# An SSD mixer's elementwise work is moved from GpSimd to VectorE and ScalarE, and its norm's sums to other banks

## The chip, the cores and the metric

The program runs on one core of a Trainium2 chip. The metric is device time in microseconds (us). In the profile PE is the matrix engine, PEld its weight load, DVE the vector engine, ACT the scalar engine, POOL is GpSimd, and SP issues most of the DMAs. Each engine takes its instructions in order; they wait for each other through semaphores.

## The reference

A two-layer decoder on 1040 tokens of 1024 channels (16 learned tokens and 1024 inputs). Layer 0 is a state-space mixer (SSD) with a gated norm, layer 1 an attention; a convolutional feed-forward stands behind each. All is float32. The mixer, cut:

```python
z, xbc, dt_raw = jnp.split(u @ w_in, [...], axis=-1)
xbc = jax.nn.silu(_causal_dwconv(xbc, conv_w, conv_b))          # width 4
xs, b_in, c_in = jnp.split(xbc, [...], axis=-1)                 # 4 groups, 8 heads each
dt = jax.nn.softplus(dt_raw + dt_bias)
xdt = x_c * dt_c[..., None]
a_cs = jnp.cumsum(dt * a, axis=-1)                              # per chunk and head
decay_in = jnp.exp(jnp.where(causal, a_cs[..., :, None] - a_cs[..., None, :], -jnp.inf))
y_diag = einsum('bclgn,bcsgn->...', c_c, b_c) * decay_in @ xdt
chunk_states = einsum(b_c, jnp.exp(a_cs[..., -1:] - a_cs), xdt)
state = state * chunk_decay + chunk_states                      # from chunk to chunk
y = y_diag + einsum(c_c, prev_state, jnp.exp(a_cs)) + xs * d_skip
hg = y * jax.nn.silu(z)                                         # per group of 512 channels
hg = hg * lax.rsqrt(jnp.mean(hg * hg, -1) + eps) * gate_g
h = h + hg @ w_out
```

## The kernel before

Every matmul in float32 is done as three products of rounded halves (`mm3`: hi by hi, hi by lo, lo by hi); the high half `wh` of a weight block comes from ACT, the low half `wl = w - wh` from another engine (`load_w`). Channels lie on the 128 partitions, tokens along the free axis in three tiles of 348, 348 and 344 (`TT`).

The mixer (0 to about 660 us of the span) first normalizes the input, makes `dt` and its running sums (`dt_path`, a generator whose steps are called between projection tiles) and projects group 0. Then four groups with nine chunks of 116 tokens each follow. For each chunk `ssd_decays` loads the running sums `D` (116 x 8 heads x 116) and `E`, takes differences and the exponential, and multiplies E by C; `ssd_front` makes C·B (`cb`), transposes x (`px`) and B (`pb`, copied by ACT to `bk`), and multiplies `xdt`, `D`, `xde`; `ssd_back` makes the chunk's state `S`, updates `state`, and makes `y`, which is added to x. Between a chunk's front and back stand tiles of projection work for the next groups, 24 products of 3 x 8 each (`stream`): the six conv blocks of the next group (`in_group`; a tile ends with ACT's L273 and three DVE L277, all reading the PSUM bank), and the four gate blocks of the present one (`gate_group`; ACT's silu reads the bank, then DVE multiplies). A block's weights are loaded when the block before it begins. When a group's gate blocks are through, its gated norm (`gate_norm`) is called once ahead of each of three tiles that follow: a matmul with ones sums the squares over channels into a bank `ms`, then come Ln, Exp, one Newton step on DVE, and four scalings.

PSUM has eight banks: `mm` has two and `ex` one, between which projection tiles rotate (the third tile of a block takes `ex`), `sm` has three (cb, pb, y, ms), `lg` two (px, S). A bank comes free when its last reader is done.

In this section the order of PE, DVE, ACT and POOL is the order in which the code is written (`manual_schedule`); SP's DMAs, and the rest of the kernel except the attention, are ordered by the framework's scheduler. Behind the section the output projection (`out_proj`, accumulators `acc`, result added to `h` on DVE) begins, and the last group's norm sums stand among its first products.

The norm's sums and steps, which several places share:

```python
def rstd(self, accs, n, width, y=None, table=True):            # L178
    if table:
        self.ln_exp()                                          # ACT table load
    ps = self.sm("ms")
    ... matmul(ps, ones, acc)                                  # L187
    nc.scalar.activation(y, ps, AF.Ln, scale=1.0 / width)      # L190
    nc.scalar.activation(y, y, AF.Exp, scale=-0.5)             # L191
    b = y * y; b = b * ps; b = -0.5 / width * b + 1.5; y = y * b   # DVE, L192 to L195
```

Of the kernel before, what the change touches and what calls it, by code (L numbers as in the profile page):

```python
# [8 lines left out]
F32 = mybir.dt.float32  # L9
F32R = mybir.dt.float32r  # L10
AF = mybir.ActivationFunctionType
ALU = mybir.AluOpType
# [30 lines left out]
SMB, LGB = 3, 2  # L43
DT0 = 0
LAG = 2

NW = 8
SUMS = ((6, 1), (3, 6), (7, 6), (3, 5), (5, 7)), ((4, 7), (2, 1))
# [19 lines left out]
class Trunk:  # L68
# [64 lines left out]
                                pattern=[[1, CB]], channel_multiplier=-1)  # L133


    def load_w(self, src, n, gain=None, pool=None, tags=("wh", "wl"), eng=None):
        nc = self.nc
        pool = pool or self.wp
        w32 = self.wp.tile([P, 1024], F32, tag="w32", name=self.nm("w32"))
        nc.sync.dma_start(w32[:, :n], src)  # L140
        if gain is not None:
            v = w32[:, :n].rearrange("p (k c) -> p k c", k=KD)
            g = gain.unsqueeze(2).to_broadcast([P, KD, n // KD])
            nc.gpsimd.tensor_tensor(v, v, g, op=ALU.mult)
        wh = pool.tile([P, 1024], F32R, tag=tags[0], name=self.nm("wh"))
        wl = pool.tile([P, 1024], F32R, tag=tags[1], name=self.nm("wl"))
        nc.scalar.activation(wh[:, :n], w32[:, :n], AF.Copy)
        (eng or nc.gpsimd).tensor_tensor(wl[:, :n], w32[:, :n], wh[:, :n].bitcast(F32), op=ALU.subtract)
        return wh, wl

    def mm3(self, out, wh, wl, uh, ul, first, last, joins=False):
# [363 lines left out]

    def gate_norm(self, g, x, acc, j):
        s0, n = TT[j]
        r = self.rstd([acc.pop(j)], n, DI // GROUPS)
        for q in range(4):
            xq = x[q][:, s0 : s0 + n]  # L520
            self.nc.vector.scalar_tensor_tensor(xq, xq, self.par("gate_norm", 4 * g + q), r, op0=ALU.mult, op1=ALU.mult)

    def settle(self):

# [30 lines left out]
    def ssd_decays(self, g, ct, c, pool):  # L555

        nc = self.nc
        h0 = GH * g
        t0, n = CH[c]
        cc = 3 * (c % 3) + c // 3  # L560
        dk = pool.tile([P, 1024], F32, tag="D", name=self.nm("D"))
        dk = dk[:n, : GH * CB].rearrange("p (h l) -> p h l", h=GH)
        nc.sync.dma_start(dk, self.acs_d[c, h0 : h0 + GH].unsqueeze(0).to_broadcast([n, GH, CB]))
        dk = dk[:, :, :n]
        ce = None
        if c:
            ce = pool.tile([P, GH * CB], F32, tag="E", name=self.nm("E"), bufs=2)
            ce = ce.rearrange("p (h l) -> p h l", h=GH)
            nc.sync.dma_start(ce, self.ea_d[c, h0 : h0 + GH].unsqueeze(0).to_broadcast([P, GH, CB]))
            ce = ce[:, :, :n]  # L570
        yield dk, ce

        for i in range(GH):
            nc.vector.tensor_scalar(dk[:, i], dk[:, i], self.cols[:n, 1, cc, h0 + i : h0 + i + 1], 0.0, op0=ALU.subtract, op1=ALU.min)
        nc.scalar.activation(dk, dk, AF.Exp)
        yield
        if c:
            nc.gpsimd.tensor_tensor(ce, ce, ct[:, t0 : t0 + n].unsqueeze(1).to_broadcast([P, GH, n]), op=ALU.mult)
        yield

    def ssd_front(self, g, x, bt, ct, c, dk, pool):

        nc = self.nc
        h0 = GH * g
        tt = nc.vector.tensor_tensor
        t0, n = CH[c]
        cc = 3 * (c % 3) + c // 3
        e = t0 + n
        pcb = self.sm("cb")
        nc.tensor.matmul(pcb[:n, :n], bt[:, t0:e], ct[:, t0:e], start=True, stop=True)  # L590
        px = self.lg("px")
        for q in range(4):
            nc.tensor.transpose(px[:n, q * P : q * P + P], x[q][:, t0:e], self.ident)
        px = px[:n].rearrange("p (h d) -> p h d", h=GH)
        cbm = pool.tile([P, CB], F32, tag="cbm", name=self.nm("cbm"), bufs=2)
        tt(cbm[:n, :n], pcb[:n, :n], self.past[:n, :n], op=ALU.mult)
        xdt = pool.tile([P, GH, 64], F32, tag="xdt", name=self.nm("xdt"), bufs=2)
        tt(xdt[:n], px, self.cols[:n, 0, cc, h0 : h0 + GH].unsqueeze(2).to_broadcast([n, GH, 64]), op=ALU.mult)
        tt(dk, dk, cbm[:n, :n].unsqueeze(1).to_broadcast([n, GH, n]), op=ALU.mult)
        bk = xde = None  # L600
        if c < 8:
            pb = self.sm("pb")
            nc.tensor.transpose(pb[:n, :P], bt[:, t0:e], self.ident)
            bk = pool.tile([P, P], F32, tag="bk", name=self.nm("bk"), bufs=2)
            nc.scalar.activation(bk[:n], pb[:n, :P], AF.Copy)
            xde = pool.tile([P, GH, 64], F32, tag="xde", name=self.nm("xde"), bufs=2)
            nc.gpsimd.tensor_tensor(xde[:n], xdt[:n], self.cols[:n, 2, cc, h0 : h0 + GH].unsqueeze(2).to_broadcast([n, GH, 64]), op=ALU.mult)
        return xdt, xde, bk

    def ssd_back(self, g, x, c, dk, ce, xdt, xde, bk, state, pool):  # L610

        nc = self.nc
        h0 = GH * g
        t0, n = CH[c]
        cc = 3 * (c % 3) + c // 3
        e = t0 + n
        new = None
        if c < 8:
            ps = self.lg("S")
            nc.tensor.matmul(ps, bk[:n], xde[:n].rearrange("p h d -> p (h d)"), start=True, stop=True)  # L620
            new = pool.tile([P, GH, 64], F32, tag="state", name=self.nm("state"), bufs=2)
            psv = ps.rearrange("p (h d) -> p h d", h=GH)
            if c == 0:
                nc.scalar.activation(new, psv, AF.Copy)
            else:
                nc.gpsimd.tensor_tensor(new, state, self.cd[:, cc, h0 : h0 + GH].unsqueeze(2).to_broadcast([P, GH, 64]), op=ALU.mult)
                nc.vector.tensor_tensor(new, new, psv, op=ALU.add)
        py = self.sm("y")
        for i in range(GH):
            q, r = i // 2, 64 * (i % 2)  # L630
            y = py[r : r + 64, q * CB : q * CB + n]
            nc.tensor.matmul(y, xdt[:n, i, :], dk[:, i, :], start=True, stop=c == 0)
            if c:
                nc.tensor.matmul(y, state[:, i, :], ce[:, i, :], start=False, stop=True)
        for q in range(4):
            nc.vector.scalar_tensor_tensor(x[q][:, t0:e], x[q][:, t0:e], self.par("d_skip", 4 * g + q),
                                           py[:, q * CB : q * CB + n], op0=ALU.mult, op1=ALU.add)
        return new

    def mixer(self, mx):  # L640
# [5 lines left out]
        with self.tc.tile_pool(name="ssd", bufs=3) as pool:  # L646
# [17 lines left out]
            into = lambda g: self.in_group(u, g, rows[g])  # L664
            blocks = into(1) + gate(0) + into(2) + gate(1) + into(3) + gate(2) + gate(3)
            for n, _ in enumerate(self.stream(into(0))):
                if n % 3 == 2:
                    next(dt, None)
                if n == 14:
                    w0 = self.load_w(blocks[0][0], D)  # L670
            work = self.stream(blocks, w0)
            E = mybir.EngineType
            with self.tc.manual_schedule(engines={E.PE, E.DVE, E.Activation, E.Pool}):
                ahead = self.ssd_decays(0, rows[0][5], 0, pool)
                dk, ce = next(ahead)
                for g in range(GROUPS):
                    *x, bt, ct = rows[g]
                    tiles, given = (18, 30, 30, 18)[g], 0
                    state = None
                    for c in range(9):  # L680
                        for _ in ahead:
                            pass
                        ops = self.ssd_front(g, x, bt, ct, c, dk, pool)
                        now = dk, ce
                        for _ in range((tiles * (c + 1) + 8) // 9 - given):
                            next(work)
                            if given == (tiles * c + 8) // 9:
                                nxt = (g, ct, c + 1) if c < 8 else (g + 1, rows[g + 1][5], 0) if g < 3 else None
                                ahead = self.ssd_decays(*nxt, pool) if nxt else iter([(None, None)])
                                dk, ce = next(ahead)  # L690
                            else:
                                next(ahead, None)
                            given += 1
                        state = self.ssd_back(g, x, c, *now, *ops, state, pool)
                        if g == 3:
                            done.append(c)
                            todo, waiting[:] = waiting[:], []
                            for w in todo:
                                later(*w)
# [4 lines left out]
    def out_proj(self, hd, ys, yd, pool):  # L704
# [3 lines left out]
        for g in range(3):  # L708
            ops = [self.split(ys[g][q] if yd[g] is None else self.fetch(yd[g][q], "y"), "y") for q in range(4)]
            for f in range(KD):  # L710
                w = self.load_w(a["w_out_f"][g, f], 4 * P, eng=self.nc.vector)
                if g == 0:
                    h[f] = self.fetch(hd[f], "h", front=HB)
                for s0, n in TT:
# [712 lines left out]
    def o_proj(self, hd, od, pool):  # L1427
# [14 lines left out]
        ops = [[x[:, ORG:L] for x in self.split(self.fetch(od[p], "o"), "o")] for p in range(first - 2)]  # L1442
        ops = [ops + [part(p, 0) for p in (first - 2, first - 1)], ops]
        for f in range(KD):
            w = self.load_w(a["w_o_f"][f], first * P, eng=self.nc.vector)
            h[f] = self.Q("h")
            self.nc.sync.dma_start(h[f][:, : L - ORG], hd[f, :, ORG:])
            for j in range(4):
# [152 lines left out]
```

## Time and profile before

| what | value |
|---|---|
| time, median of 3 runs | 2941.55 us (2941.41 to 2942.75) |
| the profiled execution: its own time, its span | 2945.51 us, 2943.8 us |
| granted PE clock over the span | 0.988 |
| busy: PE, DVE, ACT, POOL | 2844.7, 2162.0, 1616.7, 964.3 us |
| POOL's weight splits L148 in the mixer | 40, 96.5 us |
| POOL's E products L578, xde L607, state L626 | 32, 32, 28: 72.8, 60.0, 32.8 us |
| DVE's differences L574 | 288, 91.6 us |

The profiled execution took 4.0 us longer than the median of the runs, and its span is 1.7 us shorter than its own time. In a row of a timeline stand the start, the duration (of a run of equal instructions, from the first start to the last end), the engine, the line, the operation with its tiles (result, arrow, operands), and in brackets how long the engine had been idle and whose end released it. In an answer on waits stand the total, the number of times and the longest.

### The profile page before, as it was taken

The page shows a single profiled execution, that of the slowest core. Times are in us where ns is not written, and L with a number is a line of the kernel's source. Part 1 is how long each engine was busy: PE and PEld are TensorE (multiplying, and loading weights), DVE is VectorE, ACT ScalarE, POOL GpSimd, SP SyncE. Part 2 cuts the span into 40 slices and gives each one's busy share as a digit, 9 for nine tenths or more (in the row PEclk, how much of TensorE's full clock was granted, in tenths as well). Part 3 has the DMA queues.
Part 4 walks back from the last instruction along what each step waited for, and adds up shares of the span by engine and source line. Part 5 has one row for each costly group of instructions (what it writes and reads, how often), then busy time and mean ns, then how long its engine had stood idle before and what let it go on. Part 6 is the DMA issues. An engine that isn't in the chain of part 4 may idle for free.

```text
span 2943.8 us, 57054 instructions
## 1 busy us (share of the span) xinstructions
PE 2844.7 (97%) x21781; PEld 2714.2 (92%) x21781; DVE 2162.0 (73%) x4222; ACT 1616.7 (55%) x3302; POOL 964.3 (33%) x1088
## 2 busy tenths in 40 slices
PE   7999999989998999999999999999898999999998
PEld 4999898979998999999999999999798999999888
DVE  5677868895578565558986888888869656557895
ACT  4554555553246555555334888878736555555442
POOL 1253444450004666660002222222200766662000
PEclk9999999999999999999999999999998999999999
DMA  5233333323231222226132222222341222225331
GB/s 165 77 103 92 107 91 103 104 73 135 63 111 55 80 80 80 80 80 216 54 136 75 60 60 65 64 60 63 99 146 64 84 80 78 82 80 186 107 108 58
DMA packets 128962, 272.74 MB, mean 93 GB/s; under 512 B 15888, under 2 KB 59536, under 8 KB 128688
## 3 DMA queue, kind: packets, MB, share of 16 engines
q1 hardware_dynamic: 123376, 258.17, 27.2%
q10 hardware_dynamic: 4048, 6.36, 0.6%
q0 software_dynamic: 1264, 4.57, 0.4%
q8 instruction: 171, 2.80, 0.4%
q14 instruction: 103, 0.84, 0.1%
HBM read 200.93 MB, written 53.21 MB: 86 GB/s over the span
## 4 chain that ended last, share of the span: by engine, by line
PE 80%; DVE 10%; ACT 5%; issue 2%; POOL 2%; DMA 2%; SPq 0%; DVEq 0%; ACTq 0%; POOLq 0%
PE p L154 10%; PE p L156 10%; PE p L155 10%; PE acc L155 8%; PE acc L156 8%; PE acc L154 8%; PE pj L154 6%; PE pj L155 5%; PE pj L156 5%; PE po L1355 2%; PE lg L1313 2%; PE wT L1340 1%; DVE kp L1326 1%; ACT kp L1316 1%; ACT bt L1317 1%
## 5 line engine op out<-in xcount | busy, mean ns | idle before, releaser
L154 PE MATMUL pj<-uh,wh 128*128 128x348 f32 (+2 forms) x1536 | 506.5, 330 | 14.8 <-DVE qs L1264 7.2
L155 PE MATMUL pj<-ul,wh 128*128 128x348 f32 (+2 forms) x1536 | 498.4, 324 | 0.0
L156 PE MATMUL pj<-uh,wl 128*128 128x348 f32 (+2 forms) x1536 | 495.8, 323 | 0.0
L154 PE MATMUL p<-bh,fh 128*128 128x262 f32 (+1 forms) x1408 | 401.3, 286 | 4.8 <-ACT ft L947 2.9
L155 PE MATMUL p<-bl,fh 128*128 128x262 f32 (+1 forms) x1408 | 401.4, 286 | 3.0 <-DVE bl L847 3.0
L156 PE MATMUL p<-bh,fl 128*128 128x262 f32 (+1 forms) x1408 | 400.4, 285 | 0.0
L154 PEld LDWEIGHTS pj<-uh,wh 128*128 128x128 f32 x1536 | 291.8, 190 | 21.8 <-DVE qs L1264 9.5
L155 PE MATMUL p<-bl,wh 128*128 128x262 f32 (+1 forms) x1056 | 301.1, 285 | 5.1 <-DVE bl L847 5.1
L154 PE MATMUL p<-bh,wh 128*128 128x262 f32 (+1 forms) x1056 | 301.8, 286 | 3.9 <-ACT bh L846 3.3
L156 PE MATMUL p<-bh,wl 128*128 128x262 f32 (+1 forms) x1056 | 301.6, 286 | 0.0
L155 PEld LDWEIGHTS pj<-ul,wh 128*128 128x128 f32 x1536 | 292.3, 190 | 1.4 <-issue 0.5
L156 PEld LDWEIGHTS pj<-uh,wl 128*128 128x128 f32 x1536 | 291.7, 190 | 0.3 <-issue 0.2
L900 POOL TENSOR_TENSOR fl<-x,fh 128x1024 fp32r<-128x1024 f32 x80 | 192.4, 2406 | 253.7 <-ACT fh L899 253.7
L154 PEld LDWEIGHTS p<-bh,fh 128*128 128x128 f32 x1408 | 268.8, 191 | 6.4 <-ACT ft L947 3.6
L277 DVE SCALAR_TENSOR_TENSOR c<-p,params,c 128x260 f32<-128x260 f32 (+1 forms) x440 | 208.0, 482 | 89.6 <-ACT c L273 87.7
L155 PEld LDWEIGHTS p<-bl,fh 128*128 128x128 f32 x1408 | 268.7, 191 | 4.6 <-DVE bl L847 4.4
L156 PEld LDWEIGHTS p<-bh,fl 128*128 128x128 f32 x1408 | 268.1, 191 | 0.1
L950 DVE TENSOR_TENSOR p<-p,ft 128x262 f32<-128x262 f32 (+1 forms) x176 | 76.6, 436 | 217.8 <-ACT ft L947 124.8
L155 PE MATMUL acc<-gl,wh 128*128 128x260 f32 (+1 forms) x672 | 211.3, 320 | 0.2
L156 PE MATMUL acc<-gh,wl 128*128 128x260 f32 (+1 forms) x672 | 208.7, 320 | 0.0
L155 PEld LDWEIGHTS p<-bl,wh 128*128 128x128 f32 x1056 | 202.5, 192 | 6.0 <-DVE bl L847 6.0
L154 PEld LDWEIGHTS p<-bh,wh 128*128 128x128 f32 x1056 | 202.5, 192 | 4.6 <-ACT bh L846 3.5
(317 smaller groups left out, 7926.9 us busy)
## 6 DMA issues: line engine op xcount, KB each, us to landing
w<-in_w_up SPq DMA_DIRECT2D x88, 512.0 KB
w<-in_w_down SPq DMA_DIRECT2D x44, 512.0 KB
w<-in_w_in SPq DMA_DIRECT2D x40, 512.0 KB
E<-ea_d SPq DMA_DIRECT2D x32, 464.0 KB
D<-acs_d SPq DMA_DIRECT2D x32, 420.5 KB
g<-c SPq DMA_DIRECT2D x88, 130.0 KB
g<-c SPq DMA_DIRECT2D x88, 128.0 KB
b<-g SPq DMA_DIRECT2D x16, 520.0 KB
```

Source lines behind the costliest of these rows:

```text
L154: mm(out, wh, uh, start=first, stop=False, skip_group_check=joins)
L155: mm(out, wh, ul, start=False, stop=False, skip_group_check=joins)
L156: mm(out, wl, uh, start=False, stop=last, skip_group_check=joins)
L277: nc.vector.scalar_tensor_tensor(to, ps[:, o + i : o + i + n], wcol(i), out, op0=ALU.mult, op1=ALU.add)
L900: tt(lo[:, :n], t, hi[:, :n].bitcast(F32), op=ALU.subtract)
L950: add = lambda o, x, y: tt(o[:, :N], x[:, :N], y[:, :N], op=ALU.add)
L1313: nc.tensor.matmul(ps[:nt, :m], part[:, c0 : c0 + nt], ks[a][:, s0 : s0 + m], start=x == 0, stop=x == 1)
L1316: nc.scalar.activation(kp[:nt, :m], ps[:nt, :m], AF.Sigmoid, scale=self.rt[2][:nt, i : i + 1])
L1317: nc.scalar.activation(bt[:nt, :m], ps[:nt, :m], AF.Sigmoid, scale=self.rt[1][:nt, i : i + 1])
L1326: nc.vector.tensor_tensor_scan(rev, rev, self.one[:nt].to_broadcast([nt, m + 1]), init, ALU.mult, ALU.mult)
L1340: nc.tensor.transpose(pt[:ns, x * CB : x * CB + nt], bt[a][:nt, x * CB : x * CB + ns], self.ident[:nt, :nt])
L1355: nc.tensor.matmul(po[64 * a : 64 * a + 64, w], v[: CH[c][1], c, 64 * a : 64 * a + 64], wt[a][: CH[c][1], c, :nt], start=x == 0, stop=x == ...
```

## The change

- `load_w` gives every `wl` to DVE (L148); 40 in the mixer were POOL's. So go E by C (L578), `xde` (L607) and the state's decay (L626). POOL keeps no arithmetic in this section, only the issue of the stores of y.
- The differences (L574), eight per chunk on DVE as subtract and min, become eight ACT Relu with scale −1 and the running sum as bias, and the exponential gets the scale −1.
- `gate_norm` does its own norm: the sum goes to the bank `ex` for the first tile and `mm` for the other two, ACT copies it to SBUF at once, and all that follows reads the copy.
- Two tiles of work are issued ahead of the first chunk (`EARLY`), so that group 0's chunks hold 16 rather than 18, and the steps of `dt_path` are called at tiles 1, 3, 5 rather than 2, 5, 8.

```diff
-        (eng or nc.gpsimd).tensor_tensor(wl[:, :n], w32[:, :n], wh[:, :n].bitcast(F32), op=ALU.subtract)
+        nc.vector.tensor_tensor(wl[:, :n], w32[:, :n], wh[:, :n].bitcast(F32), op=ALU.subtract)
...
     def gate_norm(self, g, x, acc, j):
         s0, n = TT[j]
-        r = self.rstd([acc.pop(j)], n, DI // GROUPS)
+        nc, width = self.nc, DI // GROUPS
+        tt = nc.vector.tensor_tensor
+        v, r = acc.pop(j)[:, :n], self.tmp("y")[:, :n]
+        ps = (self.mm if j else self.ex)("ms")[:, :n]
+        nc.tensor.matmul(ps, self.ones, v, start=True, stop=True)
+        nc.scalar.activation(v, ps, AF.Copy)
+        self.ln_exp()
+        nc.scalar.activation(r, v, AF.Ln, scale=1.0 / width)
+        nc.scalar.activation(r, r, AF.Exp, scale=-0.5)
+        for _ in range(2):
+            tt(v, v, r, op=ALU.mult)
+        nc.vector.tensor_scalar(v, v, -0.5 / width, 1.5, op0=ALU.mult, op1=ALU.add)
+        tt(r, r, v, op=ALU.mult)
         for q in range(4):
             xq = x[q][:, s0 : s0 + n]
...
         for i in range(GH):
-            nc.vector.tensor_scalar(dk[:, i], dk[:, i], self.cols[:n, 1, cc, h0 + i : h0 + i + 1], 0.0, op0=ALU.subtract, op1=ALU.min)
-        nc.scalar.activation(dk, dk, AF.Exp)
+            nc.scalar.activation(dk[:, i], dk[:, i], AF.Relu, scale=-1.0, bias=self.cols[:n, 1, cc, h0 + i : h0 + i + 1])
+        nc.scalar.activation(dk, dk, AF.Exp, scale=-1.0)
         yield
         if c:
-            nc.gpsimd.tensor_tensor(ce, ce, ct[:, t0 : t0 + n].unsqueeze(1).to_broadcast([P, GH, n]), op=ALU.mult)
+            nc.vector.tensor_tensor(ce, ce, ct[:, t0 : t0 + n].unsqueeze(1).to_broadcast([P, GH, n]), op=ALU.mult)
...
-            nc.gpsimd.tensor_tensor(xde[:n], xdt[:n], ...)
+            tt(xde[:n], xdt[:n], ...)
...
-                nc.gpsimd.tensor_tensor(new, state, ...)
+                nc.vector.tensor_tensor(new, state, ...)
...
             for n, _ in enumerate(self.stream(into(0))):
-                if n % 3 == 2:
+                if n in (1, 3, 5):
                     next(dt, None)
...
+                for _ in range(EARLY):
+                    next(work)
                 for g in range(GROUPS):
-                    tiles, given = (18, 30, 30, 18)[g], 0
+                    tiles, given = (18 - EARLY, 30, 30, 18)[g], 0
```

Lines of the changed kernel are one higher than before up to the norm, 13 higher from the differences on. DVE ahead of the first norm (`z` are gate tiles and, squared and summed, the norm's input; `xbc` the group's channels). Before:

```order
L599 TENSOR_TENSOR D_2644<-D_2644,cbm_2757 116x928
L510 TENSOR_TENSOR z_2314<-z_2314,z_2718 128x348
L499 TENSOR_TENSOR xbc_886<-xbc_886,z_2793 128x348
L510 TENSOR_TENSOR z_2347<-z_2347,z_2793 128x348
L499 TENSOR_TENSOR xbc_886<-xbc_886,z_2827 128x344
L574 TENSOR_SCALAR D_2798<-D_2798,cols 116x116 x8
L510 TENSOR_TENSOR z_2385<-z_2385,z_2827 128x344
L277 SCALAR_TENSOR_TENSOR xbc_2847<-pj_2848,params,xbc_2847 128x348 x3
```

The same place on DVE after:

```order
L612 TENSOR_TENSOR D_2644<-D_2644,cbm_2757 116x928
L620 TENSOR_TENSOR xde_2766<-xdt_2759,cols 116x512
L511 TENSOR_TENSOR z_2314<-z_2314,z_2718 128x348
L500 TENSOR_TENSOR xbc_886<-xbc_886,z_2793 128x348
L511 TENSOR_TENSOR z_2347<-z_2347,z_2793 128x348
L500 TENSOR_TENSOR xbc_886<-xbc_886,z_2827 128x344
L149 TENSOR_TENSOR wl_2844<-w_376_2841,wh_2843 128x1024
L511 TENSOR_TENSOR z_2385<-z_2385,z_2827 128x344
L278 SCALAR_TENSOR_TENSOR xbc_2847<-pj_2848,params,xbc_2847 128x348 x3
L591 TENSOR_TENSOR E_2800<-E_2800,xbc_2090 128x928
```

The eight differences are gone, and xde, a weight split and the E product have come in; the conv steps L278 of the tile `pj_2848` now stand behind the weight split. On ACT at the same place, after:

```order
L505 ACTIVATE z_2793<-xbc_886 128x348
L587 ACTIVATE D_2798<-D_2798,cols 116x116 x8
L588 ACT_TABLE_LOAD
L588 ACTIVATE D_2798<-D_2798 116x928
L148 ACTIVATE wh_2843<-w_376_2841 128x1024
L274 ACTIVATE xbc_2847<-pj_2848,params 128x348
L505 ACTIVATE z_2827<-xbc_886 128x344
L524 ACTIVATE z_2314<-ms_2881 128x348
L179 ACT_TABLE_LOAD
```

The eight Relu stand ahead of the table load and the exponential, and the weight's high half behind them; before, this was the same row of work without the Relu, and Ln read `ms` where the copy does now. On PE, where the last projection tile ends and the output projection begins, before:

```order
L156 MATMUL pj_6538<-uh_142,wl_6384 128x344
L154 MATMUL acc_6670<-yh_6623,wh_6663 128x348
L155 MATMUL acc_6670<-yl_6624,wh_6663 128x348
L156 MATMUL acc_6670<-yh_6623,wl_6664 128x348
L154 MATMUL acc_6670<-yh_6633,wh_6663 128x348
L155 MATMUL acc_6670<-yl_6634,wh_6663 128x348
```

And after:

```order
L157 MATMUL pj_6547<-uh_142,wl_6393 128x344
L523 MATMUL ms_6580<-z_6057,ones 128x348
L523 MATMUL ms_6595<-z_6106,ones 128x348
L155 MATMUL acc_6784<-yh_6635,wh_6777 128x348
L156 MATMUL acc_6784<-yl_6636,wh_6777 128x348
L157 MATMUL acc_6784<-yh_6635,wl_6778 128x348
```

Two of the last group's sums now stand ahead of the first accumulator rather than behind its products.

More of the change, by code (lines that the diff above doesn't have):

```diff
@@ L45 @@
 LAG = 2
+EARLY = 2
 NW = 8
@@ L133, in consts, with load_w @@
                                 pattern=[[1, CB]], channel_multiplier=-1)
-    def load_w(self, src, n, gain=None, pool=None, tags=("wh", "wl"), eng=None):
+    def load_w(self, src, n, gain=None, pool=None, tags=("wh", "wl")):
         nc = self.nc
@@ L517, in gate_norm @@
         s0, n = TT[j]
-        r = self.rstd([acc.pop(j)], n, DI // GROUPS)
+        nc, width = self.nc, DI // GROUPS
[11 more added lines that the diff above has]
+        tt(r, r, v, op=ALU.mult)
         for q in range(4):
             xq = x[q][:, s0 : s0 + n]
-            self.nc.vector.scalar_tensor_tensor(xq, xq, self.par("gate_norm", 4 * g + q), r, op0=ALU.mult, op1=ALU.mult)
+            nc.vector.scalar_tensor_tensor(xq, xq, self.par("gate_norm", 4 * g + q), r, op0=ALU.mult, op1=ALU.mult)
     def settle(self):
@@ L606, in ssd_front @@
             xde = pool.tile([P, GH, 64], F32, tag="xde", name=self.nm("xde"), bufs=2)
-            nc.gpsimd.tensor_tensor(xde[:n], xdt[:n], self.cols[:n, 2, cc, h0 : h0 + GH].unsqueeze(2).to_broadcast([n, GH, 64]), op=ALU.mult)
+            tt(xde[:n], xdt[:n], self.cols[:n, 2, cc, h0 : h0 + GH].unsqueeze(2).to_broadcast([n, GH, 64]), op=ALU.mult)
         return xdt, xde, bk
@@ L625, in ssd_back @@
             else:
-                nc.gpsimd.tensor_tensor(new, state, self.cd[:, cc, h0 : h0 + GH].unsqueeze(2).to_broadcast([P, GH, 64]), op=ALU.mult)
+                nc.vector.tensor_tensor(new, state, self.cd[:, cc, h0 : h0 + GH].unsqueeze(2).to_broadcast([P, GH, 64]), op=ALU.mult)
                 nc.vector.tensor_tensor(new, new, psv, op=ALU.add)
@@ L710, in out_proj @@
             for f in range(KD):
-                w = self.load_w(a["w_out_f"][g, f], 4 * P, eng=self.nc.vector)
+                w = self.load_w(a["w_out_f"][g, f], 4 * P)
                 if g == 0:
@@ L1444, in o_proj @@
         for f in range(KD):
-            w = self.load_w(a["w_o_f"][f], first * P, eng=self.nc.vector)
+            w = self.load_w(a["w_o_f"][f], first * P)
             h[f] = self.Q("h")
```

## The prediction

> **What bounds the kernel now.** I read the page first, then busy time by stretch, then what PE waits for inside the SSD section (100 to 660 us of the span), then the timelines round those waits.
>
> ```profile
> PE 2844.7 (97%) x21781; PEld 2714.2 (92%) x21781; DVE 2162.0 (73%) x4222; ACT 1616.7 (55%) x3302; POOL 964.3 (33%) x1088
> ```
> ```profile
> 290.00:340.00 50.00, 44.05 (x305) 40.02 (x304) 43.99 (x84) 28.48 (x38) 22.78 (x15) 0.93 0.34 110
> 440.00:500.00 60.00, 54.53 (x364) 50.11 (x363) 51.75 (x99) 30.90 (x43) 26.50 (x18) 0.91 0.35 115
> 610.00:660.00 50.00, 39.81 (x311) 35.05 (x310) 43.95 (x88) 30.47 (x43) 23.93 (x12) 0.93 0.16 51
> 100.00:660.00 560.00, 534.53 (x3911) 498.17 (x3910) 438.77 (x899) 300.35 (x428) 251.89 (x135) 0.98 0.33 97
> ```
> ```profile
> PE pb L603 <- DVE z L193: 6.9, 3, 2.6
> PE ms L187 <- ACT bk L605: 6.6, 3, 5.8
> PE pj L154 <- ACT bk L605: 5.6, 2, 3.0
> PE S L620 <- POOL xde L607: 3.3, 4, 1.3
> PE pj L154 <- DVE xbc L277: 1.6, 1, 1.6
> PE y L632 <- DVE D L599: 1.5, 1, 1.5
> ```
>
> PE is the bound, 97% of the span. The windows' columns are length, then PE, weight load, DVE, ACT and POOL busy, then granted clock, DMA share and GB/s. PE lacks 560 − 534.5 = 25.5 us in the section, and the waits add up to the same 25.5. Most sit in three stretches where a group's gated norm is worked off (290–340, 440–500, 610–660); DVE is 86 to 88% busy there. A long wait costs again afterwards:
>
> ```profile
> 327.48 0.32 PE L155 MATMUL pj<-ul,wh 128*128 128x352 f32 x1
> 327.64 0.32 PE L156 MATMUL pj<-uh,wl 128*128 128x352 f32 x1
> 330.98 0.63 PE L154 MATMUL pj<-uh,wh 128*128 128x352 f32 x1 [3.03 <-ACT bk L605]
> 331.41 0.49 PE L155 MATMUL pj<-ul,wh 128*128 128x352 f32 x1
> 331.70 0.49 PE L156 MATMUL pj<-uh,wl 128*128 128x352 f32 x1
> ```
>
> Starts are 0.16 us apart before the wait and 0.29 behind it; for some ten matmuls that is 10 × 0.13, about 1.4 us with the slow first. Five waits are that long (two in each of the first two stretches, the 5.8 in the last): 7 us. So the section can give at most 25.5 + 7 = 32.5 us, 1.1% of the kernel. The page "TensorE: Matmul & The Clock Gate" of the Trainium skill (Part 1) lowers the clock after at least one idle window of about 3.4 us; by that four of the five drops would not exist and the ceiling would be near 27. The rows show the drop after 3.03 us, so the row decides.
>
> **DVE after the change.** POOL's arithmetic goes to DVE, and its differences go to ACT. Prices:
>
> ```profile
> L1046 DVE TENSOR_TENSOR wl<-w,wh 128x1024 fp32r<-128x1024 f32 x56 | 68.4, 1223 | 11.4 <-ACT wh L1045 10.6 <-DMA g<-c 0.6
> ```
> ```profile
> L574 DVE TENSOR_SCALAR D<-D,cols 116x116 f32<-116x116 f32 (+1 forms) x288 | 91.6, 389 | 4.6 <-DMA D<-acs_d 4.6
> L499 DVE TENSOR_TENSOR xbc<-xbc,z 128x348 f32<-128x348 f32 (+1 forms) x40 | 47.4, 1184 | 15.1 <-ACT z L492 15.1
> L599 DVE TENSOR_TENSOR D<-D,cbm 116x928 f32<-116x928 f32 (+1 forms) x36 | 42.0, 1167 | 0.0
> ...
> L598 DVE TENSOR_TENSOR xdt<-px,cols 116x512 f32<-116x512 f32 (+1 forms) x36 | 24.5, 681 | 0.2 <-PE px L593 0.2
> ```
> ```profile
> 311.88 2.39 POOL L148 TENSOR_TENSOR wl<-w,wh 128x1024 fp32r<-128x1024 f32 x1 [0.82 <-ACT wh L147]
> ```
> ```profile
> 311.85 4.28 DVE L521 SCALAR_TENSOR_TENSOR xbc<-xbc,params,y 128x348 f32<-128x348 f32 x4
> ```
>
> Added: 36 weight splits × 1.22 = 44; 32 E products at the price of L599, 37; 32 xde and 28 state products at L598's 0.68, 41: together 122 us. Removed: 91.6 of differences. The last two rows show another saving: while POOL's wl ran, DVE's four scalings took 4.28 us, where four take 2.06 elsewhere (row at 302.55 below). With POOL doing no arithmetic in the section that goes; L499's 40 at 0.52, a quarter of that 2.06, would save 27 of 47. DVE: 439 + 122 − 92 − 27 = 442, 79% of the section, less if other locked operations recover too. It does not become the bound on average. In order of place:
>
> A. Two tiles before the first chunk cover the one wait on L277: −1.6 (0 to −1.6).
>
> B. S waits four times, 3.3 us, for xde, which POOL multiplies; on DVE it takes 0.68 and stands directly behind the D product. Where DVE itself is late, 0.3 of it stays: −3.0 (0 to −3.3).
>
> C. The first two norm stretches. Before, idle there is 6.0 and 5.5 plus 4 × 1.4 of slow clock, 17 us. Projections rotate over three banks; the sums now stand in that rotation and the next users wait for them. For the first stretch:
>
> ```profile
> 291.23 1.28 ACT L575 ACT_TABLE_LOAD   x1
> 293.74 0.98 ACT L575 ACTIVATE D<-D 116x928 f32<-116x928 f32 x1 [1.23 <-DVE D L574]
> 294.63 1.04 ACT L147 ACTIVATE wh<-w 128x1024 fp32r<-128x1024 f32 x1
> 295.58 0.62 ACT L273 ACTIVATE xbc<-pj,params 128x348 f32<-128x348 f32 x1
> 296.10 0.48 ACT L504 ACTIVATE z<-xbc 128x344 f32<-128x344 f32 x1
> 296.60 1.28 ACT L178 ACT_TABLE_LOAD   x1
> 297.89 0.46 ACT L190 ACTIVATE y<-ms 128x348 f32<-128x348 f32 x1
> 298.38 0.49 ACT L191 ACTIVATE y<-y 128x348 f32<-128x348 f32 x1
> ```
> ```profile
> 298.40 1.80 DVE L277 SCALAR_TENSOR_TENSOR xbc<-pj,params,xbc 128x348 f32<-128x348 f32 x3
> ...
> 302.55 2.06 DVE L521 SCALAR_TENSOR_TENSOR xbc<-xbc,params,y 128x348 f32<-128x348 f32 x4
> 304.52 1.80 DVE L277 SCALAR_TENSOR_TENSOR xbc<-pj,params,xbc 128x348 f32<-128x348 f32 x3
> ```
> ```profile
> 301.46 0.32 PE L603 MATMUL pb<-ident,xbc 128*116 128x128 f32 x1 [2.56 <-DVE z L193]
> ```
> ```profile
> 1620.69 1.30 ACT L1214 ACTIVATE wh<-w,params 128x128 fp32r<-128x128 f32 x4
> 1621.86 0.45 ACT L1362 ACTIVATE o<-po 128x116 f32<-128x116 f32 x2
> ```
>
> Nothing in this section's trace is a Relu with a bias per partition. The nearest is four ACT operations with a scale per partition on 128x128, 1.17 us from start to next start: 0.29 each, 8 in 2.3 us (upper end 0.46, ACT's 128x348 rows, 3.7). ACT begins them at 290.9; table load, exp and wh follow to 296.5. DVE, in order, takes wl there (1.2), a sum (0.5) and L277 (1.8): 300.0, and only then is the second sum's bank free. PE is there at 301.46 − 2.56 = 298.9: a wait of 1. On DVE E (1.2), the norm's four steps (1.9) and four scalings (2.1) come next, then L277 (1.8): 306.9. That frees the bank of the tile behind the third sum; PE, held up by 1, has one tile of 24 × 0.16 = 3.9 to do after the second sum and is there near 304.5: a wait of 2.3. Then PE does two tiles (7.8), a chunk's S, y, cb, px (3.6) and a tile (3.9) and is near 322. DVE does the chunk (state 1.4, y 1.1, cbm 0.3, xdt 0.7, D 1.2, xde 0.7), the second norm (4), L277 (1.8), wl (1.2), the third norm (3.8) and the L277 that frees PE's next bank (1.8), and is near 324.5: 2.4. With one slow clock about 1 + 2.3 + 2.4 + 1.4 = 7 a stretch, 14 for both: −3. The bounds: with no wait left, −17; with every one 1 us longer and two slow clocks each, +9. I take −4, since some of DVE's unquoted locks go too.
>
> D. The last norm stretch holds 1.8 + 5.8 idle, 1.4 slow clock, and 1.5 at the final y: 10.5. Projections here are gates, whose bank ACT frees, not DVE. Going along ACT (Relu 2.3, table, exp per chunk; copy, table, Ln, Exp per norm) and DVE in the same way, PE is at the three sums at 619, 627 and 631.5, and the banks' last reads are at 611, 621 and 625; it is at the tile after the last chunk at 640.5, whose bank the third copy frees at 637. DVE has the last D product ready near 651, behind the third norm, the state, y and E, while PE is there at 648: the final y waits 3. −7 (−9 to −3).
>
> F. The handover to the output projection.
>
> ```profile
> 684.57 0.43 ACT L492 ACTIVATE z<-pj 128x344 f32<-128x344 f32 x1
> ...
> 686.98 1.28 ACT L178 ACT_TABLE_LOAD   x1
> ```
> ```profile
> 691.97 0.42 PE L154 MATMUL acc<-yh,wh 128*128 128x344 f32 x1 [1.98 <-DVE h L379]
> ```
>
> PE ends the last tile just before 684.57. Two sums now stand ahead of the output's products and hold two of the three banks until ACT copies them, at 686.98 + 0.46 and, behind a table load, Ln and Exp, 690.1. PE waits 2.5 and then 0.7, with a slow clock 4.6; the 1.98 for h then mostly goes: +2.6 (0 to +4.6).
>
> G. dt's steps two tiles earlier, and no POOL beside DVE's start: −1.5 (−3 to +1). The rest of the kernel, which PE holds at full pace, has only reorderings: 0 (±1.5).
>
> Sum: −1.6 − 3.0 − 4 − 7 + 2.6 − 1.5 = −14.5 against the profiled 2945.5, 2931.0. That execution was 4.0 above the median of the runs, so 2927.0.
>
> **The rivals.** *The banks cost all that the norm gives* (15%): with C at 0 and F at 4.6, −8.5 and 2933. The waits on conv steps behind the norm's scalings speak for it. *ScalarE is too slow* (12%): at 0.43 a Relu each chunk's exp, and wh behind it, comes 1.1 later; five waits in the stretches lengthen by that, 5.5 us, 2932.5. The busy column speaks against it: 300 + 288 × 0.29 + 12 × 0.46 = 389 us, 70% (at 0.43, 77%). "ScalarE: Activation LUTs" of the Trainium skill ("Rules for kernel authors") says that relu, max and min belong on VectorE, which speaks against the move. By its figures there for a bias operand, 0.3 us and 0.83 ns an element, an estimate is 0.40 a Relu, 115 us in all. The trace has 0.29 for the nearest form against L574's mean of 0.389, so it does not bear the rule out by that much.
>
> *Slower: weights arrive late* (7%). Weights are loaded one block ahead, three tiles of 24 × 0.16 = 3.9 us, 11.6. wh stands behind Relu, table and exp (5.6 with itself), wl behind what DVE has queued, 4 in a norm: 10.8 with its own 1.2. If each of 36 blocks waits more than 14.5 / 36 = 0.4 us, all is lost; at 1.1 it is +40 − 14.5, 2967; at 0.7, 2952. Against it: only norm stretches have such a queue.
>
> *All waits go* (13%): −1.6 − 3.3 − 15 − 9 − 1.5 = −30, 2911 to 2915. *Gains move to later waits* (8%), as a queue that only shifts by its own length would: 2936 to 2946. What remains, 45%, is my forecast, 2922 to 2932.
>
> **How the numbers follow.** A measurement tells 0.2%, 5.9 us, from no change. Under 2935.7 lie the forecast, all waits gone, and four fifths of the first two rivals: 80%. Within 0.2% the rest of these and the moved gains, 13%; slower 7%. 2913 to 2938 leaves out the slower rival, half of the best case and a part of the moved gains, 18%.
>
> **What would show it.** S's waits on xde gone; L499 uniformly near 0.52; L587 near 0.29 each; in 290–340 PE waits on L278 rather than on the norm's reads, some 6 us; none of 5.8 in 610–660; a wait of 2 to 3 ahead of L155 acc at the handover. I am wrong if PE waits for wl, if Relu takes 0.4 or more, or if the norm stretches keep their 0.93 of clock with the waits unshortened.

## The result, and the profile after

The changed kernel takes 2927.11 us (median of 4 runs, 2925.54 to 2930.57) against 2941.99 before (4 runs, 2941.41 to 2942.75): ratio 0.9948, 95% interval 0.9936 to 0.9959. The forecast was 2927.0. The sum was right and several of its terms were not; the traces show which.

The profiled execution has a span of 2928.9 us, 14.9 less than before. Busy time by stretch, columns as in the prediction:

```profile
290.00:340.00 50.00, 46.42 (x328) 42.28 (x327) 41.46 (x77) 39.33 (x69) 2.18 (x4) 0.97 0.41 128
440.00:500.00 60.00, 55.22 (x392) 50.83 (x391) 50.67 (x95) 42.62 (x76) 2.10 (x4) 1.00 0.34 108
610.00:660.00 50.00, 47.37 (x345) 44.59 (x345) 35.25 (x72) 32.54 (x62) 1.67 (x1) 0.97 0.15 46
100.00:660.00 560.00, 545.98 (x4020) 510.43 (x4019) 409.05 (x753) 390.46 (x738) 5.95 (x9) 0.99 0.34 98
```

PE lacks 14.0 us in the section (100 to 660) where it lacked 25.5. ACT's 390 is the 389 of the sum; DVE's 409 lies below its 442, since more of its operations got shorter than were counted. L500 (L499 before, 1184 ns), which was counted, is down to a quarter of the four scalings' time, as forecast (shown for 100 to 640, where this kernel has 40 of them). Its neighbour L511 (L510 before), which was not, went from 1231 to 517 ns.

```profile
L500 DVE TENSOR_TENSOR xbc<-xbc,z 128x348 f32<-128x348 f32 (+1 forms) x40 | 20.3, 512 | 14.1 <-ACT z L493 14.1
```

PE's waits in the section after, and then those at the handover (660 to 720):

```profile
PE pj L155 <- DVE xbc L278: 8.7, 6, 2.0
PE y L645 <- DVE D L612: 3.0, 2, 2.6
PE S L633 <- DVE xde L620: 1.1, 1, 1.1
PE pj L155 <- ACT xbc L274: 0.8, 1, 0.8
```
```profile
PE ms L523 <- ACT z L493: 2.6, 1, 2.6
PE acc L155 <- DVE h L380: 2.3, 2, 1.2
```

Neither the norm's reads nor bk hold PE any more; conv steps do. A table of when PE starts the same work in the two profiled executions tells where the 14.9 arose. (The first four rows are the start of the chunk's matmul `cb`, chunks counted from 0; the rows bound the places of the prediction.)

| PE starts | before, us | after | difference | gained in between |
|---|---|---|---|---|
| group 1, first chunk | 231.09 | 230.98 | −0.1 | −0.1 start and group 0 |
| group 1, chunk 8 (behind norm 1) | 373.25 | 369.36 | −3.9 | −3.8 first norm stretch |
| group 2, chunk 8 (behind norm 2) | 530.18 | 521.71 | −8.5 | −4.6 second norm stretch |
| group 3, chunk 6 | 614.59 | 602.08 | −12.5 | −4.0 waits of S |
| last rows of y | 659.38 | 639.01 | −20.4 | −7.9 last norm stretch |
| last projection product | 682.23 | 662.99 | −19.2 | +1.1 behind the final y |
| second part of the output projection (waits for yh) | 739.20 | 725.52 | −13.7 | +5.6 handover |
| end of the span | 2943.8 | 2928.9 | −14.9 | −1.2 the rest |

### The profile page after: what moved, and what is told of

It reads as the page before. It is cut to its first block, busy times and chain, and to the rows that moved or that the text cites. A ratio compares the mean times of both kernels' runs of the same rounds, so it can differ in the third digit from the quotient of the medians.

```text
span 2928.9 us, 56936 instructions
## 1 busy us (share of the span) xinstructions
PE 2841.1 (97%) x21781; PEld 2711.2 (93%) x21781; DVE 2124.2 (73%) x4066; ACT 1702.2 (58%) x3602; POOL 702.3 (24%) x956
## 4 chain that ended last, share of the span: by engine, by line
PE 67%; DVE 6%; ACT 4%; issue 1%; DMA 1%; ACTq 0%; DVEq 0%; SPq 0%; POOL 0%
PE p L156 10%; PE p L155 10%; PE p L157 10%; PE acc L156 8%; PE acc L157 8%; PE acc L155 8%; PE po L1370 2%; PE pj L155 2%; PE pj L157 2%; PE pj L156 2%; PE lg L1328 2%; PE wT L1355 2%; ACT kp L1331 1%; ACT bt L1332 1%; DVE kp L1341 1%
## 5 line engine op out<-in xcount | busy, mean ns | idle before, releaser
L278 DVE SCALAR_TENSOR_TENSOR c<-p,params,c 128x260 f32<-128x260 f32 (+1 forms) x440 | 207.9, 481 | 91.1 <-ACT c L274 89.0
```

The lines of the kernel that those rows point to most:

```text
L278: nc.vector.scalar_tensor_tensor(to, ps[:, o + i : o + i + n], wcol(i), out, op0=ALU.mult, op1=ALU.add)
```

## The experiments

Each kernel below is the changed one with the edit shown. Kernels of one set shared a chip and its runs of the kernel before; intervals are those of the ratio to before (medians 2942 to 2943). Differences of up to about 5 us between two of these kernels from different sets are within what these intervals leave open; where a smaller one is read below, it rests on the traces.

### Which part made the gain

**GpSimd's work back on GpSimd** (`undo_pool`):

```diff
-        nc.vector.tensor_tensor(wl..., op=ALU.subtract)     # the mixer's 40
+        nc.gpsimd.tensor_tensor(wl..., op=ALU.subtract)
-            nc.vector.tensor_tensor(ce, ...); tt(xde, ...); nc.vector.tensor_tensor(new, state, ...)
+            nc.gpsimd.tensor_tensor(ce, ...); nc.gpsimd... (xde); nc.gpsimd... (new, state)
```

> The changed kernel, but GpSimd keeps its arithmetic of the SSD section (the mixer's weight splits, E, xde, the state's decay). Theory 1 (GpSimd's slow operations and the lengthening of VectorE's beside them made the waits): S waits for xde again (+4), VectorE's gate products take over 1 us again, the last norm stretch and the first two lose half of their gain; 2936 to 2942 us. Rival (the sums' new banks made the gain in the norm stretches): only the 4 us at S come back, about 2931.

2939.16 us, ratio 0.9990 (0.9980 to 0.9999): 12 us of the gain gone, as theory 1 had it. By PE's starts the first two norm stretches gain 3.1 and 3.2 less than in the changed kernel, the last one 3.2 and S 2.1 less; S waits only once, 2.2 us, where theory 1 had 4. PE waits again on DVE's late operations, and DVE's are long again:

```profile
PE ms L523 <- DVE xbc L278: 5.5, 2, 2.8
PE y L645 <- DVE D L612: 5.1, 1, 5.1
```
```profile
L500 DVE TENSOR_TENSOR xbc<-xbc,z 128x348 f32<-128x348 f32 (+1 forms) x38 | 40.6, 1072 | 20.7 <-ACT z L493 20.7
```

**The weight splits alone back on GpSimd** (`undo_wl`; E, xde and state stay on DVE):

> The changed kernel with the mixer's weight splits alone back on GpSimd (40 of 2.4 us), E, xde and state on VectorE. Theory 1 (what hurts is GpSimd's reading beside VectorE, and xde and D's chain behind it): a third of GpSimd's time is back, +3 to +6, 2930 to 2933 us. Rival (the weight split in VectorE's queue, which waits up to 5 us for ScalarE's high half, is itself a burden on VectorE): 2924 to 2927.

2940.19, ratio 0.9990 (0.9981 to 1.0000). Both sides were wrong: the splits alone cost all 13 us, although they take only 86 us of POOL (100 to 640). The largest loss between two chunks, 3.5 us from the first to the second of group 3, shows how. In this kernel's POOL and DVE timelines:

```profile
549.70 2.35 POOL L149 TENSOR_TENSOR wl<-w,wh 128x1024 fp32r<-128x1024 f32 x1 [15.14 <-ACT wh L148]
```
```profile
550.20 2.83 DVE L612 TENSOR_TENSOR D<-D,cbm 116x928 f32<-116x928 f32 x1
552.95 0.68 DVE L620 TENSOR_TENSOR xde<-xdt,cols 116x512 f32<-116x512 f32 x1
```

The D product takes 2.83 us, where the changed kernel's mean is 1.11, until 1.0 us after POOL's split ends; xde behind it is late, and PE's S waits 3.58 us for it. The split can only begin when ACT's wh is done, and here that falls where DVE takes up work that PE waits for. That it is the splits' place that hurts is read from this trace; no run here has them at another place on GpSimd. The Trainium skill, page "SBUF — State Buffer", section "Who interferes with whom", has the same: a VectorE instruction with two SBUF inputs contends with a GpSimd instruction that reads SBUF. The trace agrees: 2.83 against 1.11.

**The differences back on DVE** (`undo_relu`):

```diff
-            nc.scalar.activation(dk[:, i], dk[:, i], AF.Relu, scale=-1.0, bias=...)
-        nc.scalar.activation(dk, dk, AF.Exp, scale=-1.0)
+            nc.vector.tensor_scalar(dk[:, i], dk[:, i], ..., 0.0, op0=ALU.subtract, op1=ALU.min)
+        nc.scalar.activation(dk, dk, AF.Exp)
```

> The changed kernel, but the decays' differences are on VectorE again (eight in some 1.6 us without GpSimd beside them). Theory 1 (VectorE is what PE waits for, in the conv steps): each wait on L278 grows by about 1.6, five of them and the last y: +6 to +9, 2933 to 2936 us. Rival (ScalarE's Relu chain, 2.35 us a chunk, is as late as VectorE would be): within 2 us of 2927, or below.

2939.76, ratio 0.9988 (0.9979 to 0.9998): +12.7, more than theory 1 had, and not where it had it. The waits on L278 became less (5.7 for 8.7), those on D and xde grew:

```profile
PE y L645 <- DVE D L612: 7.9, 2, 5.4
PE S L633 <- DVE xde L620: 7.2, 3, 3.8
PE pj L155 <- DVE xbc L278: 5.7, 5, 1.6
```

With 1.6 us more in DVE's queue every chunk, even the quiet group 0 waits for xde and D (3.79 and 2.53 us); at group 1's first chunk this kernel is 7.5 us behind the kernel before, which is most of the loss.

**Both back** (`undo_both`, the two edits together; banks, early tiles and dt steps are left):

> The changed kernel with GpSimd's arithmetic back on GpSimd and the differences back on VectorE: only the norm's banks, the early tiles and the dt steps are left of the change. Undoing either alone cost about 12 us. Theory (each of the two moves makes room for the other: VectorE can take GpSimd's work only without the differences): the two costs overlap, 2939 to 2944 us. Rival (independent gains): 2927 + 12 + 12.7, about 2950 to 2953.

2957.20, ratio 1.0050 (1.0033 to 1.0066). My theory of overlapping costs fell: 2927.1 + 12.0 + 12.7 is 2951.8, and it is 5 more, at the edge of what the intervals leave open. So the rest of the change alone makes the kernel before 14 us slower. In the section PE's waits add up to 25.6, as before: what the norm's reads no longer cost comes back elsewhere (one wait of 3.2 is on the sum's copy, which stands in ACT's queue behind an exp that waits for D, and holds a projection bank):

```profile
PE pj L155 <- DVE xbc L278: 6.9, 6, 1.6
PE S L633 <- POOL xde L620: 6.5, 5, 3.3
PE pj L155 <- ACT bk L618: 6.4, 2, 3.2
PE pj L155 <- ACT z L524: 3.2, 1, 3.2
```

Most of the loss lies outside the norm stretches. By PE's starts this kernel is 5.3 us behind the kernel before at group 1's first chunk, loses 5.6 from the last chunk's cb to the last y and 4.6 at the handover. Its waits there (660 to 745) begin with

```profile
PE y L645 <- DVE D L612: 5.9, 1, 5.9
PE ms L523 <- ACT z L493: 2.5, 1, 2.5
```

**The two moves alone** (`moves_alone`: the change without its new norm, early tiles and dt steps):

> Only the two moves between engines (GpSimd's arithmetic to VectorE, the differences to ScalarE); the norm's sums, the first chunk and the dt steps as before. What the two moves leave out cost 14 us on the old engines. Theory 1 (with the engines moved, banks and early tiles are nearly indifferent): undoing the banks gave 2.7, undoing the early start took 2.5, so about 2927, 2925 to 2929 us. Rival (banks and early start need each other, or hurt as they did on the old engines): 2915 to 2920.

2925.85, ratio 0.9943 (0.9927 to 0.9960), as theory 1 had it. The moves between engines are the whole gain; with them made, banks and early start add nothing in sum.

### The norm's banks

**All sums in the old bank** (`undo_bank`; `gate_norm` calls `rstd` as before):

> The changed kernel, but the norm's sums are made as before: in a bank of the chunk's pool, held until VectorE's third norm step has read it. Theory 1 (VectorE relieved is enough): PE waits on the norm's read shrink to under 1 us by themselves, and the handover to the output projection loses its 2.6 us wait; 2921 to 2924 us. Rival (the banks made the gain): the waits of 2.5 us, twice, and of 5.8 us come back less than half relieved, +8 to +12, less 5 at the handover; 2930 to 2934.

2924.42, ratio 0.9941 (0.9925 to 0.9958): the time is near theory 1's range, but its waits under 1 us are not what is seen. The norm's reads still hold PE,

```profile
PE pb L605 <- DVE z L194: 4.3, 2, 2.2
PE ms L188 <- ACT bk L607: 3.3, 3, 2.6
```

but at the first two stretches the kernel gains as much as the changed one (−4.0 and −4.6 in the table's terms). At the last one it gains 2.9 less up to the last chunk's cb, but its final y then waits 1.52 us and not 2.63, and at the last projection product the two have gained the same (6.6 and 6.7 since chunk 6 of group 3). At the handover it loses nothing.

**Only the last group's sums in the old bank** (`last_sm`):

```diff
+        if g == 3:
+            return self.gate_norm_sm(g, x, acc, j)      # the routine of before, with rstd
```

> The changed kernel, but only the last group's three sums, at the handover to the output projection, use the old routine and bank. Theory (two sums ahead of the first accumulator hold two of the three banks and cost some 5 us): the wait of 2.6 us on the sum and the slow clock behind it go, 2921 to 2923 us. Rival (the waits for h and the yh splits take the place): 2925 to 2927.

2922.53, ratio 0.9933 (0.9919 to 0.9948): −4.6, as the theory had it. The intervals alone don't tell this kernel from the changed one; the traces do. Between the last projection product and the yh wait this kernel needs 718.09 − 662.32 = 55.8 us, the changed one 62.5, the one before 57.0.

**The norm's DVE half behind the next conv steps** (`norm_split`, on top of `last_sm`): `gate_norm` returns its DVE steps, and `stream` runs them when the tile is issued.

> The changed kernel with the last group's sums in the old bank, and the VectorE half of the other norms (four steps, four scalings) issued behind the conv steps of the tile that follows, not ahead of them. Theory (PE waits in the norm stretches because the conv steps stand behind the norm's 4 us on VectorE): the waits on L278, 7.6 us, fall under 3; 2916 to 2919 us. Rival (VectorE is simply full there, so the waits move to xde, D or y): 2921 to 2923.

2925.84, ratio 0.9943 (0.9928 to 0.9957): 3.3 above `last_sm`, which the intervals leave open. My theory fell: by PE's starts the first two norm stretches gain what they gain in `last_sm` (3.9 and 4.5 against 3.8 and 4.4), and the final y waits 4.41 us for 2.61. The rival holds: the waits move. The first conv wait (304.90 in `last_sm`) is gone, and others come in. From this kernel's PE timeline:

```profile
323.28 0.40 PE L155 MATMUL pj<-uh,wh 128*128 128x352 f32 x1 [1.50 <-DVE xbc L278]
...
329.11 1.10 PE L645 MATMUL S<-xde,bk 116*128 116x512 f32 x2 [1.72 <-DVE xde L632]
...
345.81 0.40 PE L155 MATMUL pj<-uh,wh 128*128 128x348 f32 x1 [1.32 <-DVE xbc L278]
```

DVE is busy for 42.0 of the 50 us from 290 to 340 here; this other order only chose who is late.

### The early start

**Without early tiles and earlier dt steps** (`last_sm_late`), **without the dt steps alone** (`last_sm_dt`), both on `last_sm`:

> The changed kernel with the last group's sums in the old bank (2922.5 us), and without the two early tiles and the earlier dt steps. Theory (the early start gives back in waits on the conv steps what it takes away at the first chunk): within 1.5 us of 2922.5. Rival 1 (the first chunk's wait of 1.6 us and the start's 3 us come back in full): 2925 to 2927. Rival 2 (the earlier dt steps themselves made the new waits): 2920 to 2921.

> The changed kernel with the last group's sums in the old bank (2922.5 us), two early tiles kept, dt's steps where they were. Undoing both cost 2.5 us. Theory (the early tiles are the gain; the earlier dt steps only crowd VectorE in the start, where 2.1 us of new waits on L278 appear): 2920 to 2922.5 us. Rival (the early tiles need dt early, since the first chunk else waits for dt): 2924 to 2927.

2925.07 (0.9940, 0.9925 to 0.9956) and 2923.15 (0.9930, 0.9915 to 0.9945), against 2922.53. The dt steps change nothing that can be told. The tiles may be worth 2.5, between the theory and rival 1, and these runs don't settle it. What they cover has grown: without them the first chunk's wait on L278 is 4.13 us, where the kernel before had 1.62.

### A better version

**E alone back on GpSimd** (`last_sm_e`), **and the state's decay too** (`last_sm_e_st`), on `last_sm`:

```diff
-            nc.vector.tensor_tensor(ce, ce, ..., op=ALU.mult)
+            nc.gpsimd.tensor_tensor(ce, ce, ..., op=ALU.mult)
-                nc.vector.tensor_tensor(new, state, ...)         # the second kernel only
+                nc.gpsimd.tensor_tensor(new, state, ...)
```

> The changed kernel with the last group's sums in the old bank (2922.5 us), and the E products alone on GpSimd again. Returning the weight splits alone cost as much as returning all of GpSimd's work, so E, xde and state did not matter together. Theory (VectorE is full in the norm stretches; 1.1 us a chunk less helps more than GpSimd's 2.4 us beside it hurts): 2919 to 2922 us. Rival (any two-input operation of GpSimd lengthens VectorE's beside it, and what VectorE gains it loses): 2923 to 2927.

> The kernel at 2909.6 us (the change, the last group's sums in the old bank, E products on GpSimd) with the state's decay on GpSimd as well. Theory (in the norm stretches whatever leaves VectorE's queue brings PE's next bank forward, and the state is not needed before the next chunk's y): another 0.7 us a chunk there, 2905 to 2908 us. Rival (the sum of state and S on VectorE now waits in its queue for GpSimd's 1.1 us, and VectorE's two-input operations beside it get longer): 2910 to 2914.

2909.56, ratio 0.9887 (0.9872 to 0.9902), 13 us below `last_sm` where the theory had 0.5 to 3.5, and 2907.75, ratio 0.9884 (0.9868 to 0.9901), the fastest kernel of the study; the time is in the expected range, but the step from the one to the other is too small to be told by these intervals. In `last_sm` DVE's queue ahead of the second sum reads

```profile
296.19 1.80 DVE L278 SCALAR_TENSOR_TENSOR xbc<-pj,params,xbc 128x348 f32<-128x348 f32 x3
297.92 1.11 DVE L600 TENSOR_TENSOR E<-E,xbc 128x928 f32<-128x928 f32 x1
298.95 1.07 DVE L531 TENSOR_TENSOR z<-z,y 128x348 f32<-128x348 f32 x2
```

and in `last_sm_e`, on DVE and POOL,

```profile
287.17 2.50 DVE L500 TENSOR_TENSOR xbc<-xbc,z 128x344 f32<-128x344 f32 x1
292.24 1.23 DVE L149 TENSOR_TENSOR wl<-w,wh 128x1024 fp32r<-128x1024 f32 x1 [2.56 <-ACT wh L148]
```
```profile
287.08 2.23 POOL L600 TENSOR_TENSOR E<-E,xbc 128x928 f32<-128x928 f32 x1 [13.60 <-DMA E<-ea_d]
```

E on POOL waits only for its transfer, and runs long before it would stand in DVE's queue. It lengthens L500 here to 2.50 as well, but DVE has to wait for wh afterwards anyway, so that costs nothing at this place. (Like the D product above, L500 ends soon after POOL's operation, 289.67 after 289.31, nearly as if it had begun only then.)

The gain is more than E's own 1.11 us: the conv steps L278 begin at 293.81 and not at 296.19. In `last_sm` the E of the chunk before (281.73, 1.12 long) also stands ahead of DVE's L500, for whose result ACT's square waits 1.97 us, until 288.60; behind the square ACT makes the Relu, the exponential and wh. In `last_sm_e` this wait is gone, and wh begins 2.4 us earlier (291.16 for 293.55). So what leaves DVE's queue counts again through ACT's. PE's whole list of waits in `last_sm_e_st` (100 to 660), 4.8 us where `last_sm` has 12.8:

```profile
PE pj L155 <- DVE xbc L278: 1.5, 3, 0.6
PE y L654 <- DVE D L621: 1.0, 1, 1.0
PE pj L155 <- ACT xbc L274: 0.8, 1, 0.8
PE S L642 <- ACT xbc L274: 0.8, 1, 0.8
PE acc L155 <- DVE h L380: 0.7, 2, 0.4
```

With all waits that short the clock stays at 1.00 in the three stretches, where `last_sm` has 0.97.

## Why the prediction was right, and where it was not

The forecast's kind and size held: −14.9 of span for −14.5. Term by term:

- **A and G, the start: −3.1 forecast, −0.1 measured.** The wait named went (1.6 at the first chunk), and two in the start with it (1.4 and 1.7). What failed is that nothing was put in their place: new waits of 1.33, 0.18, 0.60 and 0.80 us on conv steps and 1.09 on xde appear before 190 us, 4.0 together. The runs tell their causes apart. The 1.33 stands in `undo_wl` and `undo_pool` too, which have the splits on GpSimd, and not in the kernels with dt's steps where they were: it is the price of the earlier steps, whose reciprocal of 1.94 us stands among the conv steps on DVE. (With dt late and the splits on DVE, as in `last_sm_dt`, a wait of 1.18 comes instead.) The next three are gone in `undo_wl` and `undo_pool`: they come with wl, whose price had been counted in DVE's busy time only, not in its queue. The 1.09 stays in `undo_wl` (1.04) and is gone in `undo_pool`: it comes with xde, E and the state on DVE.
- **B, S and xde: −3.0 forecast, −4.0 measured.** Right in its mechanism: the four waits, 3.3 together, are gone. Where the other 0.7 comes from stays open.
- **C, the first two norm stretches: −4 forecast, −8.4 measured.** The mechanism was the one named: waits on L278 where the norm's scalings stand ahead of the conv steps, at the second and third of the three places (1.52 and 1.94 for 2.3 and 2.4). The first wait, of 1, did not come, since DVE reached the conv steps at 297.09, not near 298.2. The slow clock was mis-sized: set at 1.4 a stretch, it was seen behind one of these four waits. A later wait of 1.17 (499.89) was not foreseen. What is left in the two stretches is 8.1 of waits and this 1.4, where the term had 14.

```profile
305.80 0.40 PE L155 MATMUL pj<-uh,wh 128*128 128x352 f32 x1 [1.52 <-DVE xbc L278]
...
323.14 0.40 PE L155 MATMUL pj<-uh,wh 128*128 128x352 f32 x1 [1.94 <-DVE xbc L278]
```

- **D, the last norm stretch: −7 forecast, −7.9 measured**, with 2.63 at the final y for 3. Right, by its steps: the three sums start at 606.7, 614.7 and 619.0, which, with the 12.5 us that the kernel is ahead by then, are the 619, 627 and 631.5 that were worked out. The slow clock behind the final y's wait takes 1.1 back by the last projection product, which no term had. The experiments give this to the engine moves: at that product `undo_bank`, with the old banks, has gained the same.
- **F, the handover: +2.6 forecast, +5.6 measured.** A wait of 2.60 us came, for 2.5, and the slow clock behind it, but not for the reason given. The term had PE wait behind the sums, until ACT has copied them. The trace has it wait ahead of them: the first sum takes the bank `ex`, which holds the last gate tile until ACT's silu has read it, and that stands behind splits of yh and a wh. So the near agreement in size is luck. The credit failed too: the wait for h (1.98 before) did not go but became two of 1.17 and 1.16.

```profile
665.91 2.69 PE L523 MATMUL ms<-z,ones 128*128 128x348 f32 x4 [2.60 <-ACT z L493]
```
```profile
665.42 0.43 ACT L493 ACTIVATE z<-pj 128x344 f32<-128x344 f32 x1
```

- **Prices.** A Relu lasts 0.378 us; as they overlap, the 288 took 84.7 us of ACT, 0.294 each, and eight in a row 2.35. The scale-per-partition rows were the right neighbour, and the rival of a slow ScalarE fell. The prediction's comparison of 0.29 with L574's 0.389 was of unlike things, the spacing of starts and the length of one operation; L574's 288 took 91.6 us, 0.318 each. The rule of the Trainium skill that the prediction cites against the move, relu on VectorE ("ScalarE: Activation LUTs", "Rules for kernel authors"), would here have cost 12.7 us (`undo_relu`), since it puts 57.5 us back into VectorE's queue.
- **Rivals.** Weights late: PE waited nowhere for wl, though DVE stood 40.5 us waiting for wh (100 to 640). That the banks cost all that the norm gives is what the experiments come nearest to: in the changed kernel they are worth nothing in sum.

That the number fell within 0.2 us is luck. C, B and D gained 4.4, 1.0 and 0.9 more than forecast, 6.3 together; A with G gained 3.0 less, F lost 3.0 more, beyond its own range, and the 1.1 behind the final y was not foreseen: 7.1. What the rest of the kernel gave, −1.2, was set at nothing (±1.5). The sign and the size of the change come from mechanisms that the runs bear out; the close hit comes from errors that cancel.

## What to carry to other kernels

In these runs, moving work between engines is priced by the queue it enters at the place where the bound engine waits, not by busy time: one weight split beside a D product made that product 1.7 us longer just where PE waited for it, while an E product that runs whenever its transfer lands is best left on GpSimd, where it takes twice as long (2.23 us for 1.11). Give an otherwise idle engine the work with slack, and keep from it what must run beside the critical engine. Parts of a change have to be tried together and apart: two moves, each worth 12 in the changed kernel, carried a rest that alone would have cost 14.

## What was not expected of the hardware

The matmuls slow down behind shorter gaps than the 2.5 us that the prediction went by, and not always. The kernel before has it already, outside the section: behind its wait of 1.98 us for h (691.97) the starts come to be 0.29 us apart. In the changed kernel the matmuls behind a wait of 1.94 us at 323.14 come to be 0.29 us apart, while behind one of 1.96 at 475.65 they stay at 0.16; in `last_sm` it is the one of 1.98 at 322.25 that is followed by ten slow ones at once, and in `undo_bank` a wait of 2.55 at 615.94 by none. No wait up to 1.62 us was followed by a slow clock in tile work.

```profile
475.65 0.40 PE L155 MATMUL pj<-uh,wh 128*128 128x352 f32 x1 [1.96 <-DVE xbc L278]
475.89 0.32 PE L156 MATMUL pj<-ul,wh 128*128 128x352 f32 x1
```
```profile
322.25 0.61 PE L155 MATMUL pj<-uh,wh 128*128 128x352 f32 x1 [1.98 <-DVE xbc L278]
322.66 0.50 PE L156 MATMUL pj<-ul,wh 128*128 128x352 f32 x1
```

The Trainium skill's page "TensorE: Matmul & The Clock Gate" (Part 1) tells of a free-running window; that one gap counts and the next of the same length does not would fit it. Its idle window of about 3.4 us as a condition does not fit these drops. What decides between two such gaps no run here shows.
